# A feed-forward down product computed in seven block products, with the sums of its weights made by DMA beforehand

## The chip, the cores and the metric

The kernel runs on one core of a Trainium2 chip. The metric is the time of one execution on the device in microseconds. The median of three runs of the kernel before is 3528.7 us (3525.08 to 3528.71).

## What is computed

Three transformer-like blocks run one after the other on a sequence of 1024 tokens with 1024 features, all in 32-bit floating point. Each ends in a feed-forward part, called f1, f2 and f3 here. The change touches that of the third block, f3, whose reference is cut to this:

```python
h = rms_norm_3(x, norm2_pre)               # and a modulation of its rows
f = jnp.square(jax.nn.relu(h @ w_fc1)) @ w_fc2     # 1024 -> 4096 -> 1024
x = x + g2 * rms_norm_3(f, norm2_post)     # g2: a gate per feature
```

The product with `w_fc1` is called up, that with `w_fc2` down.

## The kernel before

**Products.** Every 32-bit operand is split into a high and a low part: ScalarE copies the high part (`whi` or `Hh`, line 319) and VectorE subtracts it from the operand to give the low part (`wlo` or `Hl`, line 305). A product is then three matmuls, high by high, high by low and low by high (`mm3`, line 324). A tile of 128 by 1024 numbers, 512 KB, is one unit.

**The stream of units.** The object `W` holds all weights in the order in which they are wanted. SyncE's queue loads units into four buffers named `raw` (`drop_raws` leaves two of them), two units ahead of the split; the split writes them into six slots in SBUF. A unit is split as soon as a slot is free, and its `raw` buffer is free after that.

**Up (`up7`, line 896).** The product is cut into 2 by 2 blocks and made from seven block products in place of eight. Sums of weight blocks are made on VectorE in the `raw` buffers (`raw<-raw`), sums of the input blocks beforehand (`t`). There are 16 groups for f3. The first product of the first 12 (`FIRST`) is made in a loop ahead and kept in DRAM (`sd`), so 60 matmuls are left in each of these groups and 84 in the last four. The results of a group are four tiles of 128 by 512 in 8 slots of `X`; ScalarE applies relu and square to each and writes it to DRAM (`gd`) through its own DMA queue. GpSimd's queue brings the kept products back (line 963, `X<-sdf`). Four banks of PSUM hold the products (`mm`).

**Down (`down7`, line 1028).** For f3 the 32 tiles of `gd` come back as units and are split into `Hh` and `Hl`. They are worked off in chunks of 2, 2 and seven times 4 tiles (`CHUNKS`). Per chunk there are 8 column blocks and two halves of the tokens; VectorE adds each result to `X` (`X<-X,mm`). In the last chunk the second half of the tokens is cut in two quarters (`PARTS`), each followed by its own `tail`: the norm, the gate, the residual `xr` (read back from DRAM, `xd`) and the store of the output on SyncE's queue.

**The order.** A scheduler orders the instructions of each engine by priorities; the order on an engine is not that of the source. Each engine runs its list in order and stops where a semaphore is not there yet. `W.tick` is called all along the source; `pe` is a count of TensorE time kept while the program is built.

Of the kernel before, what the change touches and what calls it, by code (L numbers as in the profile page):

```python
# [57 lines left out]

def _feat(a):

    return np.ascontiguousarray(a.T.reshape(KT, P, a.shape[0]).transpose(1, 0, 2))


def lay_out(i):
# [42 lines left out]
    a["w3_down"] = i["w_fc2_3"].reshape(32, P, D)  # L107
# [40 lines left out]
class Stream:  # L148
# [5 lines left out]
    def __init__(self, k):  # L154
        self.k = k
        self.seq = []
        self.nd = self.ns = 0
        self.free = {"A": 4, "B": 0}
        self.pools = {}
        self.bphase = ()  # L160
        self.raws = []
        self.groom = [False, False]
# [40 lines left out]
    def _split(self):  # L203
# [38 lines left out]
        while self.nd < min(self.ns + 2, len(self.seq)):  # L242
# [23 lines left out]


class Kern:
    def __init__(self, tc, a, out):
        self.tc, self.nc, self.a, self.out = tc, tc.nc, a, out  # L270
        self.bgs = []
        self.due = {}
        self.pe = 0.0
        self.clk = {tc.nc.vector: 0.0, tc.nc.scalar: 0.0, tc.nc.gpsimd: 0.0}
        self.stacks = []
        self.ada_pend = []
        self.adap = None

# [372 lines left out]

    CHUNKS = {"f1": [2, 2] + [4] * 7, "f2": [2] + [4] * 5, "f3": [2, 2] + [4] * 7}

# [4 lines left out]
    def setup(self):  # L658
# [46 lines left out]
        def ffn7(n, up, down, with_ada=0):  # L705
# [19 lines left out]
            S[n + "h"], S[n + "d"] = [], []  # L725
            gd = S[n + "x"] = self.drp.tile([a[down].shape[0], P, T], F32, name="gd" + n)
# [168 lines left out]
    def up7(self, name):  # L895
# [3 lines left out]
        gated = name == "f2"  # L899
# [7 lines left out]
        def relu2(dst, src, m, t, scale=1.0):  # L907
            self.act(dst, src, AF.Relu, scale=scale)
            self.act(dst, dst, AF.Square)
            nc.scalar.dma_start(out=gd[m, :, 512 * t:512 * t + 512], in_=dst)  # L910
# [12 lines left out]
        for g in range(0, M, 2):  # L923
# [7 lines left out]
            for i in (0, 1):  # L931
                u = first[g + i]
                self.part7(u, 512, H[1, 0], ps[i], False)
                W.done(u)
                s = scratch()
                if gated:
                    self.act(s, ps[i], AF.Copy)
                    nc.scalar.dma_start(out=cd[g + i], in_=s)
                else:
                    relu2(s, ps[i], 2 * (g + i), 0)  # L940
# [7 lines left out]
        def slot():  # L948
            n[0] += 1
            return X1[:, (n[0] - 1) % 8]  # L950
# [6 lines left out]
        def start(g):  # L957

            ca = wide() if gated else None
            s1 = None  # L960
            if g < M:
                s1 = scratch() if gated else slot()
                nc.gpsimd.dma_start(out=s1, in_=sd[g])
                if gated:
                    nc.gpsimd.dma_start(out=ca[:, :512], in_=cd[g])
            return s1, ca

        nxt = start(0)
        for g, G in enumerate(groups):
# [18 lines left out]
            if g >= M:  # L988
# [4 lines left out]
                else:  # L993
                    relu2(slot(), z, 2 * g, 0)
# [11 lines left out]
            if not gated:  # L1006
                relu2(c22, c22, 2 * g + 1, 1)
# [4 lines left out]
            else:  # L1012
                relu2(c21, c21, 2 * g + 1, 0)
# [9 lines left out]
            else:  # L1023
                relu2(v, v, 2 * g, 1)
        W.groom[1] = True
        self.ext_es.close()
        self.open_ss()

    def down7(self, name, add, tail, quarters=False):
# [4 lines left out]
        residual = 0 if name == "f3" else 4  # L1034
# [478 lines left out]
    def block2(self):  # L1513
# [243 lines left out]

        self.up7("f2")
# [268 lines left out]
    def block3(self):  # L2027
# [204 lines left out]
        self.hp, e = self.pool("hp2", 1, None, "right")  # L2232
        self.ffn_es.insert(0, e)
        ac = []

        def add(m, part, ps, first, last):
            half, c0, c1 = part
            o = c0 - half * 512
            x = self.X[half][:, m, o:o + c1 - c0]
            if first:  # L2240
                self.act(x, ps, AF.Copy)
            else:
                self.tt(x, x, ps, ALU.add)
            if last:
                if m == 0 and o == 0:
                    ac.append(self.acc())
                if m == 0 and not xr:
                    take_slots()
                self.sq_add(ac[half], x, m, o)

        xr = []

        def take_slots():

            ts = []
            for q in "AB":
                while W.free[q] and len(ts) < 8:
                    W.free[q] -= 1
                    for n in ("hi", "lo"):
                        t = W.pools[q].tile([P, UW], F32R, tag=n, name="xr").bitcast(F32)[:, :T]  # L2260
                        t = t.rearrange("p (a b) -> p a b", b=512)
                        k = len(ts)
                        self.dma(t, self.xd[:, k:k + 2, 0:512])
                        ts.extend((t[:, 0], t[:, 1]))
            xr.append(ts)

        def tail(part):
# [3 lines left out]
            if half and len(xr) < 2:  # L2271
                t = self.hp.tile([P, KT, 512], F32, tag="h0", name="xr")
                self.dma(t, self.xd[:, :, 512:])
                xr.append([t[:, k] for k in range(KT)])
# [7 lines left out]
            for k in range(KT + 1):  # L2282
# [3 lines left out]
                if k:  # L2286
                    f = self.X[half][:, k - 1, o:o + n]
                    x = xr[half][k - 1]
                    self.tt(f, f, x[:, o:o + n], ALU.add, gp if not half or k % 2 else None)
# [4 lines left out]
        self.down7("f3", add, tail, quarters=True)  # L2294
# [30 lines left out]
```

## Time and profile before

| | |
|---|---|
| median of three runs | 3528.7 us |
| profiled execution | 3526.44 us |
| its span | 3524.6 us |
| TensorE busy | 3419.4 us, 97% |
| VectorE busy | 2201.8 us, 62% |
| ScalarE busy | 1367.4 us, 39% |
| GpSimd busy | 335.8 us, 10% |
| mean rate of DMA | 120 GB/s |

The span is the time from the first to the last instruction in the profiled execution. Busy time counts instructions, not waits. The stages that matter here, by the trace: f2 up from about 1750 to 2300 us, f2 down to about 2480, the third block's other work to 2868, f3 up to 3146, f3 down to the end.

### The profile page before, as it was taken

How to read it: one execution, taken by the hardware profiler on the slowest of the kernel's cores; microseconds unless marked ns; L12 is line 12 of the kernel's file. 1: busy time of each engine (PE TensorE's matmuls, PEld its weight loads, DVE VectorE, ACT ScalarE, POOL GpSimd, SP SyncE). 2: the span in 40 equal slices, each digit the busy share in tenths (PEclk: the TensorE clock that was granted, in tenths of full speed). 3: DMA queues.
4: the chain of work that ended last, by engine and by line, in shares of the span. 5: the costliest groups of instructions: out<-in, count | busy, mean ns of one | idle time of the engine just before them, and what ended most of it. 6: DMA issues, size and time to landing. Idle time of an engine off the chain costs nothing. (4 is left out here: it accounts for less than half of the span.)

```text
span 3524.6 us, 43683 instructions
## 1 busy us (share of the span) xinstructions
PE 3419.4 (97%) x16725; PEld 2808.1 (80%) x16725; DVE 2201.8 (62%) x3747; ACT 1367.4 (39%) x2046; POOL 335.8 (10%) x368
## 2 busy tenths in 40 slices
PE   7999999999999989999999999999999999999998
PEld 7788898887888777876698788878778878877887
DVE  5456366556666574667768988867665676645444
ACT  3432244444112443555634444431332564451111
POOL 0111020000000210000020000000232410000003
PEclk9999999999999999998999999999999999999999
DMA  3111444336633186444325322274222154343222
GB/s 106 48 43 47 148 135 148 117 118 191 184 133 113 58 196 173 123 129 147 110 94 166 116 84 84 96 221 149 88 67 90 62 184 149 132 167 114 96 84 72
DMA packets 180964, 421.46 MB, mean 120 GB/s; under 512 B 18088, under 2 KB 58744, under 8 KB 180628
## 3 DMA queue, kind: packets, MB, share of 16 engines
q1 hardware_dynamic: 133044, 325.34, 28.8%
q10 hardware_dynamic: 38304, 67.13, 5.1%
q0 software_dynamic: 9408, 26.22, 3.6%
q8 instruction: 131, 2.15, 0.3%
q14 instruction: 77, 0.63, 0.1%
HBM read 304.50 MB, written 105.63 MB: 116 GB/s over the span
## 5 line engine op out<-in xcount | busy, mean ns | idle before, releaser
L324 PE MATMUL mm<-Hh,whi 128*128 128x512 f32 (+3 forms) x3632 | 1384.2, 381 | 11.7 <-DVE X L305 4.5
L324 PE MATMUL mm<-Hh,wlo 128*128 128x512 f32 (+3 forms) x3632 | 1365.6, 377 | 4.7 <-DVE wlo L305 4.7
L324 PE MATMUL mm<-Hl,whi 128*128 128x512 f32 (+3 forms) x3632 | 1369.6, 377 | 0.2 <-DVE Hl L305 0.2
L324 PEld LDWEIGHTS mm<-Hh,whi 128*128 128x128 f32 x3632 | 686.0, 189 | 155.3 <-issue 6.8
L324 PEld LDWEIGHTS mm<-Hh,wlo 128*128 128x128 f32 x3632 | 685.7, 189 | 138.5 <-DVE wlo L305 9.0
L324 PEld LDWEIGHTS mm<-Hl,whi 128*128 128x128 f32 x3632 | 686.1, 189 | 127.7 <-issue 1.4
L319 ACT ACTIVATE whi<-raw 128x1024 fp32r<-128x1024 f32 (+3 forms) x386 | 379.0, 992 | 694.6 <-PE mm L324 459.9
L305 DVE TENSOR_TENSOR wlo<-raw,whi 128x1024 fp32r<-128x1024 f32 (+3 forms) x386 | 441.7, 1151 | 193.3 <-ACT whi L319 182.8
L305 DVE TENSOR_TENSOR X<-X,mm 128x512 f32<-128x512 f32 (+1 forms) x446 | 290.3, 655 | 366.7 <-PE mm L324 362.1
L324 PE MATMUL mm<-t,whi 128*128 128x512 f32 x1296 | 408.6, 396 | 2.4 <-ACT whi L319 2.4
L324 PEld LDWEIGHTS mm<-t,whi 128*128 128x128 f32 x1296 | 242.9, 188 | 62.4 <-ACT whi L319 3.3
L324 PE MATMUL mm<-t,wlo 128*128 128x512 f32 x648 | 256.7, 396 | 1.9 <-DVE wlo L305 1.7
L319 ACT ACTIVATE Hh<-raw 128x1024 fp32r<-128x1024 f32 x86 | 89.6, 1057 | 364.8 <-PE mm L324 213.3
L321 ACT ACTIVATE X<-X 128x512 f32<-128x512 f32 (+1 forms) x226 | 151.9, 673 | 186.2 <-DVE X L310 153.7
L305 POOL TENSOR_TENSOR acc<-acc,sq 128x256 f32<-128x256 f32 (+1 forms) x108 | 115.9, 1074 | 910.0 <-ACT sq L321 906.4
L305 DVE TENSOR_TENSOR raw<-raw 128x512 f32<-128x512 f32 x216 | 145.2, 687 | 79.5 <-DMA raw<-in_w_up 77.1
L324 PEld LDWEIGHTS mm<-t,wlo 128*128 128x128 f32 x648 | 121.8, 188 | 33.4 <-DVE wlo L305 4.1
L305 DVE TENSOR_TENSOR Hl<-raw,Hh 128x1024 fp32r<-128x1024 f32 x86 | 104.6, 1222 | 56.9 <-ACT Hh L319 56.3
L310 DVE SCALAR_TENSOR_TENSOR ada<-raw,silc,ada 128x128 f32<-128x128 f32 x336 | 115.5, 350 | 8.3
L324 PE MATMUL mm<-whi,Hh 128*128 128x264 f32 (+4 forms) x336 | 111.7, 342 | 6.5 <-ACT Hh L319 2.8
L324 PE MATMUL mm<-wlo,Hh 128*128 128x264 f32 (+4 forms) x336 | 111.2, 340 | 2.4 <-DVE wlo L305 2.4
L310 DVE SCALAR_TENSOR_TENSOR X<-mm,X 128x512 f32<-128x512 f32 x108 | 74.5, 690 | 61.6 <-PE mm L324 60.1
(290 smaller groups left out, 3400.0 us busy)
## 6 DMA issues: line engine op xcount, KB each, us to landing
raw<-in_w_up SPq DMA_DIRECT2D x136, 512.0 KB
raw<-gdf SPq DMA_DIRECT2D x86, 512.0 KB
raw<-in_w_down SPq DMA_DIRECT2D x86, 512.0 KB
gdf<-X ACTq DMA_DIRECT2D x108, 256.0 KB
raw<-in_w_ada SPq DMA_DIRECT2D x48, 512.0 KB
gdf<-X ACTq DMA_DIRECT2D x22, 512.0 KB
B<-qd SPq DMA_DIRECT2D x36, 256.0 KB
A<-qd SPq DMA_DIRECT2D x36, 256.0 KB
```

The lines of the kernel that those rows point to most:

```text
L305: eng.tensor_tensor(out=out, in0=a, in1=b, op=op)
L310: self.nc.vector.scalar_tensor_tensor(out=out, in0=a, scalar=s, in1=b, op0=op0, op1=op1)
L319: self.nc.scalar.activation(out, in_, f, scale=scale, **kw)
L321: self.nc.scalar.activation(out, in_, f, bias=bias, scale=scale, **kw)
L324: self.nc.tensor.matmul(out, l, r, start=s, stop=e, skip_group_check=grp)
```

## The change

Only the down product of f3 is put differently, with what it needs ahead of it.

- `w_fc2` is laid out by 2 by 2 blocks (`_quarters`). The product is made from seven block products, P1, P2, P6, P7, P4, P5 and P3 in this order, each in 8 steps of 24 matmuls; in each step a unit of weights and a unit of the activations are streamed and split. P1 with P2, P6 with P7 and P5 with P3 share their sums in PSUM (`down_parts`). VectorE and ScalarE touch a result only at a product's last step. The stream may run four units ahead in place of two, except in P3.
- Four of the products want sums of weight blocks. `sums` makes these in DRAM, one each 24 us of counted time from f2's up stage on: 16 copies of 1 MB from DRAM to DRAM on ScalarE's queue, kept in source order there, and 16 accumulating DMAs of 1 MB on GpSimd's queue.
- Four of the products want sums of activations. `up7` makes these for f3 with four more VectorE operations per group and writes four tiles per group through GpSimd's queue; one tile that ScalarE wrote earlier is read back per group. Sixteen slots of `X` are used in place of eight.
- The residual is read with two DMAs of 2 MB on GpSimd's queue into `Hh` at the start of the down stage. The second half of the tokens has one tail of 512 columns in place of two of 256.

```diff
+    def sums(self, name, w, pace, at):
+        S = self.S[name + "s"]
+        late = []
+        for i, q, p in ((0, 1, 3), (1, 0, None), (2, 1, 0), (3, 2, None)):
+            for e in range(4):
+                r = slice(2 * e, 2 * e + 2)
+                self.sums_todo.append((self.nc.scalar, S[i, r], w[e, q], {}))
+                self.sums_todo += late
+                src = w[e, p] if p is not None else S[0 if i == 1 else 1, r]
+                late = [(self.nc.gpsimd, S[i, r], src, dict(accum_op=ALU.add, max_dma_last_dim=4096))]
+        self.sums_todo += late
...
+    def sums_step(self):
+        if self.sums_todo and self.pe >= self.sums_at:
+            eng, dst, src, kw = self.sums_todo.pop(0)
+            ins = eng.dma_start(out=dst, in_=src, **kw)
+            if not kw:
+                self.tc.keep_in_program_order(ins)
+            self.sums_at = self.pe + self.sums_pace
...
     def tick(self):
         self.k.ada_flush()
+        self.k.sums_step()
...
+                elif parts:
+                    nc.gpsimd.dma_start(out=ca, in_=piece(0, g))
...
-                relu2(v, v, 2 * g, 1)
+                if parts:
+                    relu2(v, v)
+                    t1_, t2_, t4_ = slot(), slot(), slot()
+                    self.tt(t1_, ca, v, ALU.subtract)
+                    self.tt(v, c22, v, ALU.subtract)
+                    self.stt(t2_, t1_, -1.0, c22, ALU.mult, ALU.subtract)
+                    self.stt(t4_, t2_, -1.0, c21, ALU.mult, ALU.subtract)
+                    for i, t in ((3, t1_), (5, v), (4, t2_), (6, t4_)):
+                        nc.gpsimd.dma_start(out=piece(i, g), in_=t)
...
+    def down_parts(self, name, out, tail):
...
+        W.ahead = 4
+        new = True
+        for n, i in enumerate(self.ORDER):
+            if n == 6:
+                self.drop_raws()
+                W.ahead = 2
+            if new:
+                ps = [self.ps() for _ in range(4)]
+            for e in range(8):
+                wa, wb = (W.get(u) for u in D_[8 * n + e])
+                for m in range(4):
+                    for k in (0, 1):
+                        w, x = slice(k * 512 + m * P, k * 512 + m * P + P), slice(k * 512, k * 512 + 512)
+                        self.mm3(ps[m], wa.hi[:, w], wa.lo[:, w], wb.hi[:, x], wb.lo[:, x],
+                                 new and e == 0 and k == 0, e == 7 and k == 1, not new)
...
+                    if e == 7:
+                        z = ps[m]
+                        if i == "P1":
+                            self.act(s[:, m], z, AF.Copy)
+                        elif i == "P2":
+                            out(0, m, z, 1)
+                        elif i == "P6":
+                            self.tt(v[:, m], z, s[:, m], ALU.add)
...
+            new = i not in ("P1", "P6", "P5")
+            if i == "P4":
+                self.unsummed = True
+                self.norms[0] = self.bg(tail((0, 0, 512)))
+            elif i == "P3":
+                self.unsummed = True
+                self.norms[1] = self.bg(tail((1, 512, 1024)))
...
+        self.sums("f3", a["w3_down"], 24.0, 0.0)
         self.up7("f2")
...
         self.open_ring("f3d")
...
+        xr = self.Hh.bitcast(F32)
+        for k in (0, 4):
+            nc.gpsimd.dma_start(out=xr[:, k:k + 4, :T], in_=self.xd[:, k:k + 4])
...
-        self.down7("f3", add, tail, quarters=True)
+        self.down_parts("f3", out, tail)
```

VectorE's list in the middle of f3's up stage, one group of the kernel before. `raw<-raw` are the sums of weights, `wlo` the low parts, and `X<-mm,X` with `X<-X,mm` what becomes of the products:

```order
2690 L305 TENSOR_TENSOR raw<-raw 128x512 x2
2691 L305 TENSOR_TENSOR X_21489<-mm,X_21489 128x512
2692 L305 TENSOR_TENSOR raw<-raw 128x512
2693 L305 TENSOR_TENSOR wlo<-raw,whi 128x1024
2694 L305 TENSOR_TENSOR raw<-raw 128x512
2695 L305 TENSOR_TENSOR wlo<-raw,whi 128x1024
2696 L305 TENSOR_TENSOR X_21489<-mm,X_21489 128x512
2697 L310 SCALAR_TENSOR_TENSOR X_21489<-mm,X_21489 128x512 x2
2698 L305 TENSOR_TENSOR wlo<-raw,whi 128x512
2699 L305 TENSOR_TENSOR X_21489<-X_21489,mm 128x512
```

One group of the changed kernel at the same place, on the same engine:

```order
2650 L318 TENSOR_TENSOR raw<-raw 128x512
2651 L318 TENSOR_TENSOR X_21521<-X_21521,mm 128x512
2652 L318 TENSOR_TENSOR raw<-raw 128x512 x3
2653 L318 TENSOR_TENSOR wlo<-raw,whi 128x1024
2654 L318 TENSOR_TENSOR X_21520<-X_21520,X_21521 128x512
2655 L318 TENSOR_TENSOR wlo<-raw,whi 128x1024
2656 L318 TENSOR_TENSOR X_21520<-X_21521,X_21520 128x512
2657 L323 SCALAR_TENSOR_TENSOR X_21520<-X_21520 128x512
2658 L318 TENSOR_TENSOR X_21520<-mm,X_21521 128x512
2659 L323 SCALAR_TENSOR_TENSOR X_21520<-X_21520,X_21521 128x512
2660 L318 TENSOR_TENSOR X_21520<-mm,X_21521 128x512
2661 L318 TENSOR_TENSOR wlo<-raw,whi 128x512
```

The four new operations are those from `X` alone, without `mm`. The first addition of a product, `X<-mm,X`, stood behind two `raw<-raw` (2691) and stands behind all four, both wide `wlo` and three of the new operations now (2658).

SyncE's list where f3's up stage ends and its down stage begins, before; `in_w_up` and `in_w_down` are the weights, `gdf` the activations, and `xr` the residual:

```order
391 L183 DMA raw<-gdf_102 128x1024
392 L183 DMA raw<-in_w_up 128x1024
393 L183 DMA raw<-in_w_down 128x1024 x2
394 L183 DMA raw<-gdf_102 128x1024 x3
395 L328 DMA xr<-xd 128x8x512
396 L183 DMA raw<-in_w_down 128x1024 x2
```

The same place in the changed kernel:

```order
395 L191 DMA raw<-in_w_down 128x1024
396 L191 DMA raw<-in_w_up 128x1024
397 L191 DMA raw<-gdf_102 128x1024
398 L191 DMA raw<-in_w_down 128x1024
399 L191 DMA raw<-gdf_102 128x1024
400 L191 DMA raw<-in_w_down 128x1024
```

Weights and activations take turns now, one unit each per step, and the residual has left SyncE's list.

## Rows read from the trace of the kernel before

**Rows 1.** the page's line of engines, whole span.

```profile
PE 3419.4 (97%) x16725; PEld 2808.1 (80%) x16725; DVE 2201.8 (62%) x3747; ACT 1367.4 (39%) x2046; POOL 335.8 (10%) x368
```

**Rows 2.** windows over the down stage of f3, the first line names the columns.

```profile
core 0: us, PE busy (x) PEld busy (x) DVE busy (x) ACT busy (x) POOL busy (x), PEclk, DMA share, GB/s
3146.00:3187.00 41.00, 37.73 (x159) 29.14 (x159) 24.54 (x27) 22.52 (x31) 0.00 (x0) 1.00 0.73 255
...
3269.00:3310.00 41.00, 41.00 (x179) 33.13 (x178) 19.30 (x23) 8.16 (x8) 0.00 (x0) 1.00 0.31 103
...
3351.00:3392.00 41.00, 41.00 (x178) 33.08 (x177) 19.41 (x23) 8.15 (x8) 0.00 (x0) 1.00 0.32 103
```

**Rows 3.** waits of TensorE, f3 down; columns: us in total, times, longest.

```profile
PE mm L324 <- ACT X L319: 1.8, 1, 1.8
PE mm L324 <- DVE X L305: 1.2, 1, 1.2
```

**Rows 4.** chain of waits at the end: start, us, what.

```profile
3504.09 4.39 PE mm L324 x36
...
3518.10 0.78 DVE X L310 x2
```

**Rows 5.** windows of f2 up, f2 down and f3 up, columns as in rows 2.

```profile
1900.00:1980.00 80.00, 77.58 (x330) 60.94 (x329) 72.42 (x86) 31.95 (x31) 4.85 (x9) 1.00 0.38 125
1980.00:2060.00 80.00, 78.11 (x335) 62.46 (x334) 74.79 (x88) 36.58 (x39) 0.54 (x1) 1.00 0.29 104
2060.00:2140.00 80.00, 80.00 (x346) 64.59 (x345) 65.90 (x74) 34.08 (x37) 0.00 (x0) 1.00 0.23 79
...
2300.00:2360.00 60.00, 56.37 (x247) 44.85 (x246) 40.07 (x86) 17.33 (x19) 4.35 (x4) 1.00 0.72 205
2360.00:2420.00 60.00, 58.19 (x255) 46.85 (x254) 40.01 (x82) 10.29 (x10) 0.81 (x1) 1.00 0.65 195
...
2920.00:3000.00 80.00, 80.00 (x346) 64.47 (x345) 49.78 (x69) 37.13 (x53) 2.82 (x6) 1.00 0.46 153
```

**Rows 6.** timeline of VectorE, f3 up: start, us, operation, idle before.

```profile
2965.15 0.68 DVE L305 TENSOR_TENSOR wlo<-raw,whi 128x512 fp32r<-128x512 f32 x1
...
2969.94 1.42 DVE L305 TENSOR_TENSOR raw<-raw 128x512 f32<-128x512 f32 x2 [1.92 <-DMA raw<-in_w_up]
2971.27 0.68 DVE L305 TENSOR_TENSOR X<-mm,X 128x512 f32<-128x512 f32 x1
2971.87 0.68 DVE L305 TENSOR_TENSOR raw<-raw 128x512 f32<-128x512 f32 x1
2972.55 1.23 DVE L305 TENSOR_TENSOR wlo<-raw,whi 128x1024 fp32r<-128x1024 f32 x1
2973.69 0.68 DVE L305 TENSOR_TENSOR raw<-raw 128x512 f32<-128x512 f32 x1
```

**Rows 7.** GpSimd's sdf loads in f3 up (timeline), then that line's landing.

```profile
2916.10 0.54 POOL L963 DMA_DIRECT2D X<-sdf  x1 [39.06 <-DVE X L305]
...
3013.84 0.54 POOL L963 DMA_DIRECT2D X<-sdf  x1 [13.43 <-DMA gdf<-X]
...
DMA to landing us min/median/max: 2.7/3.2/6.2
```

**Rows 8.** accumulating loads of 1 MB, line 1066: issue in ns, landing.

```profile
L1066 POOL DMA_DIRECT2D X<-xd x8: 1273/1281/1348, 865.2 to 2359.5; - x8
...
DMA to landing us min/median/max: 10.4/13.7/17.2
```

**Rows 9.** groups by line and shape, 3146 to 3525: busy us, mean ns.

```profile
L305 DVE TENSOR_TENSOR wlo<-raw,whi 128x1024 fp32r<-128x1024 f32 x31 | 37.4, 1223 | 19.6 <-ACT whi L319 19.6
L319 ACT ACTIVATE whi<-raw 128x1024 fp32r<-128x1024 f32 x31 | 32.1, 1054 | 95.5 <-PE mm L324 66.7 <-DMA raw<-in_w_down 28.6
L310 DVE SCALAR_TENSOR_TENSOR X<-X,gp,ax 128x512 f32<-128x512 f32 x8 | 5.8, 742 | 1.2 <-PE ax L324 1.2
```

More of the change, by code (lines that the diff above doesn't have):

```diff
@@ L161, in __init__ @@
         self.raws = []
+        self.ahead = 2
         self.groom = [False, False]
@@ L241, in _split @@
         self.ns += 1
-        while self.nd < min(self.ns + 2, len(self.seq)):
+        while self.nd < min(self.ns + self.ahead, len(self.seq)):
             self.load()
@@ L905, in up7, with piece, relu2 @@
                       Hl[:, 4 * j:4 * j + 4, 512 * t:512 * t + 512]) for j in (0, 1) for t in (0, 1)}
-        def relu2(dst, src, m, t, scale=1.0):
-            self.act(dst, src, AF.Relu, scale=scale)
+        def piece(i, g):
+            if parts:
+                return gd[i, g // 2, :, g % 2]
+            h = 512 * (i > 1)
+            return gd[2 * g + (i in (1, 2)), :, h:h + 512]
+        def relu2(dst, src, i=None, g=None):
+            self.act(dst, src, AF.Relu)
             self.act(dst, dst, AF.Square)
-            nc.scalar.dma_start(out=gd[m, :, 512 * t:512 * t + 512], in_=dst)
+            if i is not None:
+                nc.scalar.dma_start(out=piece(i, g), in_=dst)
         def conv(y, c, j):
@@ L957, in start @@
         def start(g):
-            ca = wide() if gated else None
+            ca = wide() if gated else slot() if parts else None
             s1 = None
@@ L1032, in down7 @@
         D_, Gu = self.S[name + "d"], self.S[name + "h"]
-        residual = 0 if name == "f3" else 4
+        residual = 4
         c = 0
@@ L2231, in block3, with out @@
         self.open_ring("f3d")
-        self.hp, e = self.pool("hp2", 1, None, "right")
-        self.ffn_es.insert(0, e)
+        xr = self.Hh.bitcast(F32)
+        for k in (0, 4):
+            nc.gpsimd.dma_start(out=xr[:, k:k + 4, :T], in_=self.xd[:, k:k + 4])
         ac = []
[L2236 to L2241, printed above, removed]
-            else:
[L2243 to L2265, printed above, removed]
+        got = [0, 0]
+        def out(half, m, z, sign, extra=None):
+            x = self.X[half][:, m]
+            if extra is None:
+                self.act(x, z, AF.Copy)
+            elif sign > 0:
+                self.tt(x, z, extra, ALU.add)
+            else:
+                self.stt(x, z, -1.0, extra, ALU.mult, ALU.subtract)
+            if not got[half]:
+                ac.append(self.acc())
+            self.sq_add(ac[half], x, got[half])
+            got[half] += 1
         def tail(part):
@@ L2270, in tail @@
             self.unsummed = False
[L2271 to L2274, printed above, removed]
             yield self.after(1.0)
@@ L2287, in tail @@
                     f = self.X[half][:, k - 1, o:o + n]
-                    x = xr[half][k - 1]
-                    self.tt(f, f, x[:, o:o + n], ALU.add, gp if not half or k % 2 else None)
+                    self.tt(f, f, xr[:, k - 1, c0:c1], ALU.add, gp if not half or k % 2 else None)
                     self.dma(self.out[:, k - 1, c0:c1], f)
```

62 lines of the change are left out of this document (55 added, 7 removed).

## The prediction

> **What bounds the kernel now.** I began with the page's engine line: TensorE is busy 3419.4 of 3524.6 us [rows 1], so a change can pay by removing matmuls or cost by making TensorE wait; nothing else shows in the time. The table of windows over the down stage of f3, from 3146 us on, then gives the rate. Its inner rows are full, 41.00 of 41.00 us, with 178 or 179 matmuls: 82 us over 357 matmuls is 0.2297 us each [rows 2]. Only the first window is short of work, 37.73 of 41.00, with the DMA engines at a share of 0.73 [rows 2], and the view of waits names what it was: ScalarE's and VectorE's writes to X, 1.8 and 1.2 us [rows 3]. The chain of waits gives the end: the last product is the piece of 4.39 us that begins at 3504.09, so it ends at 3508.48, and after it come some 16 us of norm, residual and store, of which VectorE's last scalings, on 256 columns, take 0.39 each [rows 4]. In the windows of f3's up stage TensorE is full as well (80.00 of 80.00) while VectorE works 49.78 [rows 5]: a cover of 30 us in 80 for new VectorE work, if the order lets it be used.
>
> **What is removed.** The down product had 32 k-tiles x 8 column blocks x 2 halves x 3 = 1536 matmuls of 512 columns (the last 192 cut in 256s). Now there are 7 products x 8 steps x 24 = 1344. That is 192 fewer, all on TensorE, which is full there: 192 x 0.2297 = **-44.1 us**. The stage lasted 3508.48 - 3146 = 362.5 us against 1536 x 0.2297 = 352.8, so 9.7 us went to the first window's 3.3, the norm's small matmuls and the 256-column pieces. The pieces go, and the first two pairs of units are split before the up stage ends, since the new code may run four loads ahead. I take **-4** of these 9.7, with 0 and -9 as ends, because the residual's 4 MB now load at the same moment from GpSimd's queue.
>
> **What is added in the down stage.** Both operands are now streamed: 112 units are split where 64 were, 48 x 1054 ns more on ScalarE and 48 x 1223 on VectorE [rows 9]. Per step of 24 matmuls, 5.51 us, that is 2 x 1054 = 2.1 us and 2 x 1223 = 2.4, while the 120 additions X<-X,mm on VectorE fall to a few per product; both engines have room and I cost it at nothing. The cover is the stock of three pairs of slots (six); if it is gone, the loads set the pace, the third rival. At the end the norm's last pass is on 512 columns in place of 256. With 742 ns for a 512-wide pass [rows 9] against 0.39 [rows 4], eight of these make +2.8, the added residual on VectorE and the longer first square +1.2: **+4**, between +2 and +6. GpSimd's 512-wide residual additions run beside it.
>
> **What is added in the up stage of f3.** This is the term on which the forecast turns. Each of 16 groups gets four VectorE operations of 512 columns, four stores and one more load, the last five on GpSimd's queue, at 0.54 us of issue each [rows 7]: 6 x 0.54 = 3.2 us in a group of 13.96 (3013.84 - 2916.10 over seven issues), hidden. VectorE's load rises by 4 x 0.60 to 0.69, from about 8.7 to 11.4 us a group: still under the period. But the order says where the four stand. Before, the addition that TensorE's third block product waits for (X<-mm,X) came right behind the first two additions on raw and was done 2.0 us after the load had landed (2971.27 + 0.69 - 2969.94) [rows 6]. Now it is behind three more raw operations, two wide wlo and two of the four new ones. That closes a ring. From the end of wlo 128x512 to the landing of the next load the timeline shows 2969.94 - 2965.83 = 4.1 [rows 6]. Then follow raw 0.60, the v addition 0.60, three raw 1.80, wlo 1.14, new 0.60, wlo 1.14, new 0.60 and 0.60, the addition 0.73 (starts of neighbours in rows 6 are 0.60 apart for 512 columns, 1.14 for 1024), 12 matmuls of the third product 2.95 until its bank is read, the next addition 0.62 and wlo 0.68: 16.2 us. A group of 60 matmuls took 13.96, so 2.2 us a group where the ring is closed. By the order that holds for seven groups; 7 x 2.2 = 15, and 3 more for the groups before them, whose ring is shorter. **+18.** The upper end, if each load takes 1.5 us longer because six small transfers per group share its path (the sdf loads already land between 2.7 and 6.2 us [rows 7]), is 7 x 3.7 + 6 = +32. The lower end comes from f2, whose groups keep VectorE at 72.42 and 74.79 of 80 us and lose 2.42 and 1.89 us of TensorE, and at 65.90 (82%, what 11.4 of 13.96 would be) lose none [rows 5]: by that rate 12 groups cost between 0 and 3.0% of 168 us, 5; I set this end at +4. I take the ring, not f2's rate, since f2's order does not have the ring.
>
> The Trainium skill ("DMA: Bandwidth & Descriptors", section "Anatomy of one DMA") puts a transfer at about 2.0 us plus its bytes at 436 GB/s, written for GpSimd's queue; an estimate by that page for 512 KB is 3.2 us. The trace shows 4.1 with the wait for issue in it, on SyncE's queue, so I keep the row; by the page the ring would be 15.3 us and the term +12, the time 3499.
>
> **What is added before.** From f2's up stage on, 16 copies and 16 accumulations of 1 MB stand one every 24 us of counted TensorE time; 32 x 24 = 768 of a count that takes 0.2133 us for a matmul (512 / 2400), 827 at the trace's 0.2297. The first stand near 1890, so the last near 2720, well ahead of their first reader past 3230. The accumulation's nearest row is X<-xd, 1 MB: issue 1.28 us, landing 13.7 (10.4 to 17.2) [rows 8]. ScalarE and GpSimd lose only issue time, behind which no product waits. What they can cost is weight loads that arrive late: in f2's down stage the DMA engines are at 0.72 and 0.65 and TensorE already loses 3.63 and 1.81 us of 60 [rows 5]; about seven of the 32 fall there. The scheduler also orders f2 and block 3 slightly otherwise. Between -2 and +20, I take **+4**, near the rows' loss of 5.4 us that a busy DMA costs there today.
>
> **Sum.** -44.1 - 4 + 4 + 18 + 4 = -22.1 on the profiled execution of 3526.4 gives 3504.3; the median of the runs shown is 2.3 higher than that execution, and half of it goes on top: **3505 us**. By the low ends it is near 3480, with all high ends near 3540. About 0.2%, 7 us, is what a measurement can tell from no change, so "faster" means under 3521.6 and "slower" over 3535.8.
>
> **Rival 1, the ring is covered.** If loads land sooner or the engines run the four operations in gaps that a static order doesn't show, the up term is +4 as by f2's rows and the time 3505 - 14 = 3491. For it: VectorE idles 30 of 80 us there [rows 5]. Against: its idle time sits in front of loads and of TensorE [rows 6], where the ring has none to give.
>
> **Rival 2, the sums disturb f2.** 32 transfers of 10 to 17 us each cover about 400 us of the 827. If they hold back one load in four by another 4 us, that is 8 to 16 us in f2's up stage, where TensorE already loses 2.42 in 80 at a share of 0.38, and the loss in the down stage doubles, 5.4: +20 in place of +4, so 3521, between 3512 and 3531. For it: the windows with most DMA are those with lost TensorE time [rows 5]. Against: at 0.46, f3's up loses nothing. The Trainium skill (same page, section "Queues, rings and completion order") says that each DMA engine takes its queues in turn, packet by packet, by which a load beside a copy and an accumulation would get a third; the slower landings beside other traffic in rows 7 agree in direction, and no row has three queues at work.
>
> **Rival 3, loads set the pace of the down stage; slower than before.** A step needs 1.05 MB in 5.51 us, 190 GB/s. With four raw buffers a round of two steps is 11.03 us, of which the split holds the last buffer 1.05 + 1.22 [rows 9]; the four loads have 8.8 us, 2.10 MB, 239 GB/s. That is the point from which it decides. The first window delivered 255 [rows 2], f2's down stage 205 and 195 [rows 5]. At 205 a round takes 10.2 + 2.3 = 12.5, each of 56 steps 0.74 more, +41: 3546. Against: those rates came with the DMA engines at 0.65 to 0.73, not full, so they show what was asked for more than what can be had; the steady stage moves 103 GB/s at 0.31 [rows 2], which scales to 0.57 for 190.
>
> **Chances.** The forecast 0.48 (3497 to 3513), rival 1 0.20 (3485 to 3496), rival 2 0.17, rival 3 0.11, and 0.04 for what I have not seen, such as sums that are read before they are ready. Faster: 0.47 + 0.20 + 0.09 = 0.76. Same: 0.01 + 0.07 and 0.03 of the rest = 0.11. Slower: 0.11 + 0.01 + 0.01 = 0.13. The range 3487 to 3530 leaves out about 0.05 below and 0.13 above.
>
> **What would show it.** The distance of the group's loads on GpSimd in f3's up stage should be about 16.2 us in the seven inner groups, with TensorE waiting for X of VectorE near 2 us in each; 13.9 to 14.3 there means rival 1. The down stage should last 315 to 322 us to its last matmul, with full windows at 24 matmuls in 5.51 us and a DMA share near 0.6; waits of TensorE for whi or wlo released by DMA mean rival 3. The first of the evenly spaced loads there, at 2916.10 before [rows 7], should come within 8 us of that; 15 or more later means rival 2. The forecast fails most plainly if the up stage keeps its period, or if the inner windows of the down stage are not full.

## The result and the profile after

The changed kernel takes 3591.2 us (median of four runs, 3587.0 to 3594.1) against 3527.7 us before: a ratio of 1.018, with a 95% interval of 1.0167 to 1.0192. It is slower by 64 us; 3505 us and a gain of 22 were forecast, and the time lies outside the range. The profiled execution has a span of 3592.3 us, against 3524.6 before.

The page's line of engines answers to [rows 1]. TensorE has 288 recorded matmuls fewer and is busy 10.2 us less, not 44:

```profile
PE 3409.2 (95%) x16437; PEld 2785.2 (78%) x16437; DVE 2220.8 (62%) x3725; ACT 1407.9 (39%) x2079; POOL 396.5 (11%) x452
```

I cut both executions at the same places of the program: ScalarE's first store of `sd` in f3's up stage (2825.58 before, 2917.16 after), the first matmul of f3's down product (3146 and 3254.36), its last matmul (3508.48 and 3570.21) and the end. The store belongs to the loop that makes the first products ahead of the groups, so f3's up stage begins near 2826 in the kernel before; the 2868 given above for its start lies within it.

| from, to | before | after | difference | forecast |
|---|---|---|---|---|
| start to the first store of f3's up stage | 2825.6 | 2917.2 | **+91.6** | +4 |
| to the first matmul of the down product | 320.4 | 337.2 | +16.8 | +18 |
| to its last matmul | 362.5 | 315.9 | -46.6 | -48.1 |
| to the end of the span | 16.1 | 22.1 | +6.0 | +4 |
| sum | 3524.6 | 3592.3 | +67.7 | -22.1 |

Three of the four lines came out within 2 us. The whole miss is in the first line, in stages whose arithmetic the change does not touch.

**The down product.** The windows over it (columns as in rows 2) are full from the start; the loads delivered up to 306 GB/s where they were wanted, and settle near 186; the view of TensorE's waits has no line in this stage:

```profile
3260.00:3300.00 40.00, 40.00 (x173) 32.27 (x172) 18.31 (x16) 17.12 (x18) 0.54 (x1) 1.00 0.85 306
3300.00:3340.00 40.00, 40.00 (x173) 32.25 (x173) 17.32 (x15) 15.43 (x17) 0.00 (x0) 1.00 0.56 186
...
3500.00:3540.00 40.00, 40.00 (x173) 32.24 (x172) 26.27 (x20) 16.57 (x18) 10.17 (x6) 1.00 0.64 211
```

**Before f3.** The same kind of windows over the four stretches ahead of f3's up stage, cut at the first load of f2's down weights, the store of `xd` behind f2's down product, the first `w<-zb` of block 3 and the store named above. Before:

```profile
1840.00:2257.28 417.28, 412.97 (x1800) 332.54 (x1799) 354.02 (x411) 183.32 (x205) 14.71 (x22) 1.00 0.32 108
2257.28:2508.30 251.02, 245.14 (x1070) 197.06 (x1069) 169.54 (x316) 68.61 (x78) 9.05 (x8) 1.00 0.52 162
2508.30:2616.10 107.80, 102.01 (x439) 83.81 (x438) 67.77 (x127) 53.00 (x78) 32.87 (x28) 0.91 0.22 75
2616.10:2825.58 209.48, 206.25 (x1140) 175.27 (x1140) 118.27 (x187) 78.59 (x160) 74.46 (x78) 1.00 0.23 79
```

After:

```profile
1840.00:2295.89 455.89, 425.05 (x1807) 340.78 (x1806) 353.44 (x413) 182.89 (x207) 22.13 (x31) 0.96 0.45 136
2295.89:2567.34 271.45, 253.13 (x1067) 200.78 (x1066) 166.37 (x316) 68.60 (x78) 12.19 (x11) 0.97 0.63 180
2567.34:2700.87 133.53, 105.88 (x442) 85.90 (x441) 65.07 (x127) 55.74 (x80) 35.62 (x30) 0.83 0.31 94
2700.87:2917.16 216.29, 208.60 (x1140) 176.23 (x1140) 118.65 (x187) 77.44 (x160) 75.24 (x80) 0.99 0.31 95
```

The counts of instructions on TensorE agree within seven in each stretch, and up to that store both traces hold the same 13716 matmuls, so the work is the same. The stretches are longer by 38.6, 20.4, 25.7 and 6.8 us, which is the 91.6. TensorE's idle time (first number less second) rises from 19.2 to 84.5 us, +65.3; the other 26.3 is the matmuls taking longer, with a granted clock of 0.83 to 0.99 of full speed where it was 0.91 to 1.00.

The view of TensorE's waits from 1840 us to that store names few large ones (columns: us in total, times, longest). After:

```profile
PE ax L337 <- POOL acc L318: 18.9, 4, 17.2
PE mm L337 <- ACT whi L332: 14.2, 4, 9.1
PE mm L337 <- DVE wlo L318: 11.7, 12, 2.4
PE mm L337 <- ACT t L332: 10.5, 1, 10.5
```

Before, over the same part of the program, the first of these is small and the last does not occur:

```profile
PE mm L324 <- DVE wlo L305: 5.9, 5, 2.2
PE mm L324 <- DVE X L305: 3.3, 3, 1.5
PE ax L324 <- DVE rr L305: 2.9, 3, 1.1
PE mm L324 <- ACT whi L319: 2.4, 2, 1.3
PE ax L324 <- POOL acc L305: 2.4, 3, 1.4
```

The timeline of GpSimd shows the wait of 17.2 from the other side. Columns: start, us, engine, line, operation, and in brackets the idle time before with what ended it:

```profile
2607.24 0.45 POOL L318 TENSOR_TENSOR ws<-ws,tril 128x128 f32<-128x128 f32 x1 [43.67 <-DMA tril<-in_tril]
2607.66 1.26 POOL L318 TENSOR_TENSOR acc<-acc,sq 128x512 f32<-128x512 f32 x1
2608.87 0.46 POOL L318 TENSOR_TENSOR ws<-ws,tril 128x128 f32<-128x128 f32 x1
...
2613.14 0.90 POOL L685 DMA_DIRECT2D swf<-swf  x1
2613.75 3.26 POOL L318 TENSOR_TENSOR acc<-acc,sq 128x512 f32<-128x512 f32 x2
```

Before, the same two operations stood the other way round:

```profile
2556.65 1.72 POOL L305 TENSOR_TENSOR acc<-acc,sq 128x512 f32<-128x512 f32 x1
2558.32 2.14 POOL L305 TENSOR_TENSOR ws<-ws,tril 128x128 f32<-128x128 f32 x4
```

`ws<-ws,tril` belongs to the spatial mixing of block 3 and waits for the load of `tril`, which SyncE issued at 2601.52; `acc` is the sum of squares for which TensorE's next norm waits. In the new list `acc` stands behind it, and behind one of the new accumulations. Nothing in the diff mentions either. The scheduler had put the lists of f2 and block 3 in another order: by the two traces some 400 of the 3226 instructions of VectorE ahead of the store stand elsewhere in its list, and TensorE's list differs too. The question for the runs was how much of the 91.6 us is that order, and how much the traffic of 32 transfers of 1 MB.

### The profile page after: what moved, and what is told of

The parts are those of the page before. It is cut to its first block, busy times and chain, and to the rows that moved or that the text cites. A ratio compares the mean times of both kernels' runs of the same rounds, so it can differ in the third digit from the quotient of the medians.

```text
span 3592.3 us, 43348 instructions
## 1 busy us (share of the span) xinstructions
PE 3409.2 (95%) x16437; PEld 2785.2 (78%) x16437; DVE 2220.8 (62%) x3725; ACT 1407.9 (39%) x2079; POOL 396.5 (11%) x452
## 4 chain that ended last, share of the span: by engine, by line
PE 49%; DVE 9%; DMA 5%; issue 2%; ACT 2%; POOL 1%; SPq 0%; DVEq 0%; ACTq 0%; POOLq 0%
PE mm L337 41%; PE ax L337 5%; PE o L337 2%; DVE X L318 1%; DMA raw<-in_w_up 1%; DVE wlo L318 1%; DVE X L323 1%; DMA cb<-cs 1%; DMA raw<-in_w_ada 1%; DVE raw L318 1%; DVE ca L323 1%; POOL acc L318 1%; DVE acc L318 0%; DMA raw<-gdf 0%; DMA raw<-in_w_down 0%
## 5 line engine op out<-in xcount | busy, mean ns | idle before, releaser
L337 PE MATMUL mm<-Hh,whi 128*128 128x512 f32 (+3 forms) x3088 | 1182.5, 384 | 29.8 <-DVE X L318 16.2
L337 PE MATMUL mm<-Hh,wlo 128*128 128x512 f32 (+3 forms) x3088 | 1165.7, 378 | 14.4 <-DVE wlo L318 14.4
L337 PE MATMUL mm<-Hl,whi 128*128 128x512 f32 (+3 forms) x3088 | 1168.8, 379 | 2.3 <-DVE Hl L318 2.3
L318 DVE TENSOR_TENSOR wlo<-raw,whi 128x1024 fp32r<-128x1024 f32 (+3 forms) x466 | 544.9, 1181 | 337.3 <-ACT whi L332 331.2
L337 PEld LDWEIGHTS mm<-Hh,whi 128*128 128x128 f32 x3088 | 587.4, 190 | 156.2 <-DVE X L318 21.6
L337 PEld LDWEIGHTS mm<-Hl,whi 128*128 128x128 f32 x3088 | 587.5, 190 | 110.0 <-DVE Hl L318 3.4
L318 DVE TENSOR_TENSOR raw<-raw 128x512 f32<-128x512 f32 x216 | 143.1, 687 | 79.8 <-DMA raw<-in_w_up 78.3
L318 POOL TENSOR_TENSOR acc<-acc,sq 128x512 f32<-128x512 f32 (+1 forms) x102 | 117.0, 1148 | 682.4 <-ACT sq L334 673.9
L337 PE MATMUL mm<-whi,wlo 128*128 128x512 f32 x448 | 177.0, 395 | 0.0
L337 PE MATMUL mm<-wlo,whi 128*128 128x512 f32 x448 | 176.9, 395 | 0.0
L337 PE MATMUL mm<-whi 128*128 128x512 f32 x448 | 176.8, 395 | 0.0
```

Source lines behind the costliest of these rows:

```text
L318: eng.tensor_tensor(out=out, in0=a, in1=b, op=op)
L337: self.nc.tensor.matmul(out, l, r, start=s, stop=e, skip_group_check=grp)
```

## The experiments

In each title stands the name under which the expectation was recorded. "Store" is the first store of `sd` in f3's up stage in the profiled execution, 2825.6 before and 2917.2 after. Ratios are to the kernel before, run beside it on the same chip.

**e_nosums: the changed kernel without the sums.**

```diff
-                A.update({"P5": sw[0], "P6": sw[1], "P7": sw[2], "P3": sw[3]})
+                A.update({i: [a[down][e // 2, q, e % 2] for e in range(8)]
+                          for i, q in (("P5", 1), ("P6", 0), ("P7", 2), ("P3", 3))})
...
-        self.sums("f3", a["w3_down"], 24.0, 0.0)
```

> The changed kernel without its weight sums: no copies and no accumulations, and the four products that want sums read plain quarters of the weights in their place, so that part of the result is left out. All else is as changed, and every engine's list up to f3's up stage is that of the kernel before. By the traces the changed kernel loses 91.6 us ahead of f3's up stage, loses 16.8 in it and gains 40.6 behind it. If the sums are the whole cause of the 91.6 (theory), this kernel gives 3527.7 + 16.8 - 40.6 = 3504, within 5. If something else of the change reaches back into f2 and block 3 (rival), it stays above 3540.

3499.6 us, 0.992 [0.9902, 0.9931]; store at 2826.0; f3's up stage 336.0 us. All of the loss ahead of f3 comes with the sums, and the rest of the change saves 27 us against the kernel before beside it.

**e_before_sums: the kernel before, with the sums.**

```diff
+        self.sums("f3", a["w3_down"], 24.0, 0.0)
```

(with `sums`, `sums_step` and the DRAM they write, which no product reads)

> The kernel before with the 32 copies and accumulations added at the same pace and places, into DRAM that nobody reads. Theory, the sums alone make the loss ahead of f3: 3527.7 + 91.6 = 3619, within 8, with the losses near 1960, 2600 us. Rival, the loss comes from the sums together with the new f3 code: under 3560.

3618.7 us, 1.026 [1.0242, 1.0272]; store at 2915.2. The sums alone cost the kernel before the same 90 us, and by the traces they put its lists in the changed kernel's order up to the store.

**e_order32: the changed kernel with sums of 32 KB.**

```diff
-                self.sums_todo.append((self.nc.scalar, S[i, r], w[e, q], {}))
+                self.sums_todo.append((self.nc.scalar, S[i, 2 * e:2 * e + 1, 0:8], w[e, q][0:1, 0:8], {}))
...
```

(the accumulations likewise; the products read plain quarters as in e_nosums)

> As e_nosums, with the list of 32 copies and accumulations back but 32 KB long in place of 1 MB, read by nobody (the products read plain quarters, so that part of the result is left out). That is 1 MB of traffic where the change has 32, yet the scheduler still orders f2 and block 3 otherwise than before. Theory A, the other order makes the loss: 30 to 100 us over e_nosums, 3535 to 3605. Theory B, the traffic of the sums makes it: within 6 of e_nosums, about 3504 to 3510.

3536.3 us in one run; store at 2860.6, 35 us late with a thirty-second of the bytes. The smaller transfers also changed the scheduler's order once more, so this run says that order matters, not how much. The next two pin the order.

**x_order_before: all of the sums' bytes, in the order that the lists have with sums of 1 KB.** With 1 KB the scheduler leaves f2 and block 3 in the order of before. The kernel is built with 1 KB, its list on each engine is read off, and the full kernel is built with these lists as constraints.

```diff
+                    for p, q in zip(seq, seq[1:]):
+                        tc.add_manual_dep(traced[q], traced[p].name, mybir.DependencyInfo(
+                            mybir.DependencyClass.NoSync, mybir.DependencyReason.DATA), reason="order")
...
+    nc, order = build("tiny", None)
+    nc, got = build("full", order)
```

> The changed kernel with all its sums, 1 MB copies and accumulations that the products read, and its whole result. Only the order differs: every engine's list is the one that the scheduler gives when the same 32 transfers are 1 KB long, which up to f3 is the order of the kernel before with the transfers slipped in. Theory A, the scheduler's other order makes the loss ahead of f3: 3500 to 3510, as e_nosums. Theory B, the traffic makes it: about 3592. Mixed, 37 us of order as e_order32 had and the rest traffic: 3545 to 3560.

3512.8 us, 0.996 [0.9943, 0.9972]; store at 2837.4. The median of seven runs (3500.5 to 3520.2) is 3 us above theory A's range and far from B's. The trace bears the order out: up to the store TensorE, VectorE, GpSimd and SyncE run the same sequence as in the kernel before, the sums' transfers set aside. What the bytes still cost shows in VectorE's waits for loads in f2 (from 1840 us to just behind its down stage, 2540 and 2530; this run first, then e_nosums):

```profile
DVE raw L318 <- DMA raw<-in_w_up: 13.1, 5, 8.1
DVE raw L318 <- DMA raw<-in_w_up: 5.2, 4, 3.8
```

**x_order_after: the other corner, the changed kernel's own lists with 1 KB transfers.**

```diff
-    nc, order = build("tiny", None)
-    nc, got = build("full", order)
+    nc, order = build("full", None)
+    nc, got = build("tiny", order)
```

(against x_order_before; the products also read plain quarters as in e_nosums)

> The opposite: each engine's list word for word as in the changed kernel, but the 32 transfers 1 KB long and read by nobody (the products read plain quarters, so that part of the result is left out). Theory A, order: 3580 to 3592, the changed kernel's time nearly whole. Theory B, traffic: 3500 to 3510. Mixed: 3535 to 3560.

3571.7 us, 1.013 [1.0115, 1.0145]; store at 2899.4. That is 8 us below theory A's range and far above the others. The waits of the changed kernel are there with hardly any traffic (TensorE, from 1840 us to the store):

```profile
PE ax L337 <- POOL acc L318: 19.7, 4, 18.0
PE mm L337 <- DVE wlo L318: 12.9, 12, 2.9
PE mm L337 <- ACT whi L332: 10.0, 4, 5.7
PE mm L337 <- ACT t L332: 9.9, 1, 9.9
```

With e_nosums and the changed kernel the square is closed. Time of the store, us:

| | lists as before | lists as changed | order |
|---|---|---|---|
| next to no bytes | 2826.0 (no sums) | 2899.4 | +73.4 |
| all bytes | 2837.4 | 2917.2 | +79.8 |
| traffic | +11.4 | +17.8 | +91.2 |

Four fifths of the loss ahead of f3 is order, one fifth traffic. Each entry is one profiled execution, and executions with the same lists and bytes differ by up to 4 us at the store (2826.0 in e_nosums and 2830.3 in e_tlate below; 2837.4, 2838.9 and 2839.1 in x_order_before, c_six and c_edit2), so the traffic is known to some 4 us. The medians of the whole times give the same picture: order 72 and 78 us, traffic 13 and 20. In the left column, traffic also contains the issue of the transfers, which e_nosums doesn't have.

**a_ws: the changed kernel, block 3's `ws<-ws,tril` behind `acc`.**

```diff
+    pool = order["EngineType.Pool"]
+    ws = [n for w, g, n in Kern.MARKS if w == "ws"]
+    k = pool.index(ws[0])
+    for n in ws:
+        pool.remove(n)
+    pool[k + 14:k + 14] = ws
```

> The changed kernel in its own order of instructions, with one thing moved: the four ws<-ws,tril of block 3 stand fourteen places later in GpSimd's list, behind the additions to acc as in the kernel before, so that they no longer hold acc back while tril is being loaded. Theory (the order of the lists, not the traffic, makes block 3's start late): the wait of PE ax for POOL acc, 17.2 us from 2599 to 2617 in the changed kernel's trace, goes, and with it 17 to 25 us (the slow clock behind the gap included): 3567 to 3575 us, f3 up 17 to 25 us earlier than its 2917. Rival (the copies' traffic or another wait stands behind it): something else ends last there and the time stays within 4 us of 3591.

3588.3 us, 1.017 [1.0151, 1.0185]: a miss, the rival's figure. GpSimd's timeline shows why:

```profile
2601.01 1.27 POOL L318 TENSOR_TENSOR acc<-acc,sq 128x512 f32<-128x512 f32 x1 [30.97 <-ACT sq L334]
2610.12 0.89 POOL L695 DMA_DIRECT2D swf<-swf  x1 [7.83 <-DMA swf<-in_w_down]
2610.72 2.92 POOL L318 TENSOR_TENSOR acc<-acc,sq 128x512 f32<-128x512 f32 x2
```

One of the new accumulations stands between the additions to `acc` and waits for its copy, which ScalarE had issued at 2599.70. Two waits lay over each other, and the second took the first one's place: TensorE's wait was 16.7 us in place of 17.2.

**a_ws2: that accumulation (marked "acc" in the list) moved behind the additions as well.**

```diff
+    mv = ws + [n for n in pool[k:k + 10] if ("acc", n) in [(w, m) for w, g, m in Kern.MARKS]]
...
-    pool[k + 14:k + 14] = ws
+    pool[k + 14:k + 14] = mv
```

(against a_ws)

> a_ws with one more instruction moved: the accumulation swf<-swf that stands between the additions to acc at block 3's start, where GpSimd waited 7.83 us for its copy in a_ws (until 2610.12), goes behind them too, together with the four ws<-ws,tril. Theory (an accumulation queued on GpSimd took over the wait that the moved ws<-ws,tril gave up): PE's wait for POOL acc, 16.7 us in a_ws, goes, and 12 to 25 us with it: 3563 to 3576 us. Rival (a third thing stands behind it): within 4 us of a_ws's 3588.

3585.1 us, 1.016 [1.0145, 1.0179]; store at 2906.2. The wait of TensorE falls to 8.7 us, and what ends GpSimd's idle time there is now ScalarE's square:

```profile
2599.87 4.62 POOL L318 TENSOR_TENSOR acc<-acc,sq 128x512 f32<-128x512 f32 x3 [31.02 <-ACT sq L334]
2608.92 2.60 POOL L318 TENSOR_TENSOR acc<-acc,sq 128x512 f32<-128x512 f32 x2 [4.43 <-ACT acc L334]
```

By the median it saves 3 us against a_ws and 6 against the changed kernel, so by the time it is the rival's figure; in the profiled execution the wait is halved and the span is 10.8 us shorter than a_ws's. The stretch of block 3 is 127.3 us in place of 133.5, where it was 107.8 before. What is left may be order too, which no run isolates: TensorE's sums of squares came in two pieces with products around them before (16 matmuls at 2558.42, 16 at 2562.85), and here come as one piece of 32 with a wait on either side.

**a_t: the changed kernel, f2's four `X<-X,X` ahead of the waiting `raw<-raw`.** In the changed kernel's f2, VectorE runs the four operations that ScalarE's `t` needs only at 1900.93, behind four `raw<-raw` that waited 6.03 us for a load; before, they ran from 1864.64 on. `stt` are these four; `late` stands for the copies of ScalarE that go with them. After, then before:

```profile
1897.25 2.62 DVE L318 TENSOR_TENSOR raw<-raw 128x512 f32<-128x512 f32 x4 [6.03 <-DMA raw<-in_w_up]
...
1900.93 4.63 DVE L323 SCALAR_TENSOR_TENSOR X<-X,X 128x1024 f32<-128x1024 f32 x4
```

```profile
1864.64 1.21 DVE L310 SCALAR_TENSOR_TENSOR X<-X,X 128x1024 f32<-128x1024 f32 x1
```

```diff
...
+    for n in stt:
+        dve.remove(n)
+    j = dve.index(before[-1]) + 1
+    dve[j:j] = stt
+    late = [n for n in lo if n not in before]
+    k = act.index(late[0] - 1)
+    for n in late:
+        act.remove(n - 1)
+    act[k - 3:k - 3] = [n - 1 for n in late]
```

> The changed kernel in its own order of instructions, with one thing moved: at the start of f2's up product the four X<-X,X that ScalarE's t waits for stand ahead of the raw<-raw that waits for a load of in_w_up on VectorE, and ScalarE's four copies ahead of its whi that waits. Theory (VectorE's list holds t back): PE's wait for ACT t near 1890 to 1902 us, 10.5 us, goes, and the slow clock behind it, so f2's down product starts 8 to 20 us earlier than its 2295.89 and the time is 3571 to 3583 us. Rival (the load that comes late is needed just behind anyway, so PE waits for whi in place of t): within 4 us of 3591.

3581.2 us, 1.015 [1.0135, 1.0166]: 10 us less than the changed kernel, within what was expected. But the place is less clear than the size: TensorE still waits 5.6 us there, now for VectorE's `t`, and f2's up stretch is 450.5 us, not far below the 451.7 and 453.1 that it has in a_ws and a_ws2, where nothing was moved in it. The down stage of f2 starts 5.4 us earlier than the changed kernel's, short of the 8 to 20 expected. The wait is not gone because VectorE's own `t<-X,t`, which the edit does not move, still stand behind the load:

```profile
1893.73 2.62 DVE L318 TENSOR_TENSOR raw<-raw 128x512 f32<-128x512 f32 x4 [4.17 <-DMA raw<-in_w_up]
1896.28 1.23 DVE L318 TENSOR_TENSOR wlo<-raw,whi 128x1024 fp32r<-128x1024 f32 x1
1897.42 4.62 DVE L318 TENSOR_TENSOR t<-X,t 128x1024 fp32r<-128x1024 f32 x4
```

**a_all: both edits.**

```diff
+    pool[k + 14:k + 14] = mv
...
+    dve[j:j] = stt
...
+    act[k - 3:k - 3] = [n - 1 for n in late]
```

> a_ws2 and a_t together, whose places lie 600 us apart: if each wait is paid for by itself, the gains add, a_t's 10 us to a_ws2's 12 to 25: 3553 to 3566 us. Rival (what one saves, the other's load or copy takes back): no more than the larger of the two alone.

3582.7 us, 1.015 [1.0139, 1.0169]: the gains do not add. The rival holds, no more than the larger of the two. Both waits are as short as in the single edits (8.7 us for `acc`, 5.2 for `t`), yet f2's up stretch is 454.5 us with a_t's edit in it, no shorter than without, so a_t's gain can't be placed in that stretch; what both runs with the edit share is a shorter down stretch of f2 (267.0 and 267.4 us, where the changed kernel, a_ws and a_ws2 have 270.8 to 273.5), and why is open. So mending these two waits does not bring back the order's 73 to 80 us. That the loss is spread over many places, with a wait that goes uncovering the next, is a reading of this and not shown. Which of the many moved instructions costs what is left open.

**c_six: x_order_before, with one slot less per group in f3's up stage.** This is about the other term, +16.8 in f3. A group takes 7 of 16 slots of `X`, so the slot of the next `v` is one that the four new operations still read, and the addition for which TensorE waits cannot go ahead of them. The edit is on top of x_order_before, whose up stage lasts 331.1 us, so 6.1 of the 16.8 have gone there with the other lists.

```diff
-                    t1_, t2_, t4_ = slot(), slot(), slot()
+                    t1_, t2_, t4_ = ca, slot(), slot()
```

> As x_order_before, whole result, with one edit in f3's up stage: the first of a group's four new operations writes over the tile that was read back, so a group takes six of the 16 slots of X and not seven. With seven, the slot of a group's first addition is that of a tile which the four new operations of the group before still read, so the addition cannot stand ahead of them; with six it can, and in the list it does. Theory, the slots close the ring: groups of 14.0 to 14.8 us and 8 to 15 less than x_order_before. Rival, the work itself is too much for VectorE: period above 15.8, within 4 of x_order_before.

3505.9 us, 0.994 [0.9925, 0.9955]; f3's up stage 327.4 us. The gain of 6.9 us by the medians, 3.7 in the stage, is short of the 8 to 15 expected, and the inner groups come 15.0 us apart, between the theory's 14.0 to 14.8 and the rival's 15.8. The slot alone is a part of the cause.

**c_edit2: with the slot free, the four operations moved in VectorE's list.** The first two go behind `wlo` 128x512 of the next group, the other two behind that group's addition for `v`, in seven groups.

```diff
+        behind(t[0], dve[p])
+        behind(t[1], t[0])
+        behind(t[2], M["vadd"][g + 1])
+        behind(t[3], t[2])
```

> As c_six, with VectorE's list of seven inner groups edited: two of the four new operations stand behind wlo 128x512 and two behind the addition to v, where VectorE waits for the next load. If the ring is all that holds the groups, the period is 13.9 to 14.2 there, as before, and the time 2 to 6 below c_six; if the stores on GpSimd's queue or slower loads hold them too, no gain over c_six.

3497.4 us, 0.992 [0.9907, 0.9936]: it beats both kernels, with the whole change in it. It is 8.5 us below c_six, more than the 2 to 6 expected. The inner groups come 14.0 us apart, f3's up stage is 320.3 us, the 320.4 of before, and TensorE's longest waits from 2825 to 3254 us, which hold it, are:

```profile
PE mm L346 <- ACT whi L336: 3.4, 1, 3.4
PE mm L346 <- DVE wlo L322: 2.8, 3, 1.2
PE mm L346 <- DVE X L327: 1.9, 2, 1.0
```

**e_tlate: the same aim through the source, with the four operations written behind the next group's additions (without the sums).**

```diff
-                    self.tt(t1_, ca, v, ALU.subtract)
...
+                    late.append((g, ca, v, c22, c21))
```

> As e_nosums (plain quarters of the weights, so that part of the result is left out), with the four VectorE operations of a group in f3's up stage written behind the next group's products, so that they no longer stand ahead of the addition that TensorE waits for. If the ring makes the 16.5 us period of the changed kernel's groups (theory), the period falls to 14.0 to 14.5 and the time to 12 to 16 below e_nosums, about 3490. If VectorE's added work or the stores on GpSimd's queue make it (rival), the period stays above 15.5 and the time within 5 of e_nosums.

3506.9 us, 0.993 [0.9911, 0.9947], 7 us above e_nosums where 12 to 16 less were expected: TensorE waited 12.3 us for X, as much as the 12.2 in e_nosums. Source order does not set the list, so this run decides nothing about the ring.

## Why the prediction was wrong, point by point

**What is removed: right.** 1344 matmuls at 0.2297 are 308.7 us, and the down product lasted 315.9. The stage shrank by 46.6 for a forecast of 48.1; of the 9.7 us that it had beyond its matmuls, 7.2 stayed, so the -4 was -2.5.

**What is added in the down stage: right.** Splitting 112 units cost nothing, as the full windows show. The tail is 6.0 longer, the upper end of the 2 to 6 given. Rival 3 is refuted: its point of decision was 239 GB/s, and an early window delivered 306 with TensorE full. At a steady 186 GB/s the DMA engines are at 0.56, the 0.57 that the scaling from [rows 2] gave.

**What is added in the up stage: right, with its mechanism.** GpSimd's first stores of eight inner groups stand from 3041.05 to 3156.54, 16.5 us apart; 16.2 was worked out from the ring. TensorE's wait for X of VectorE in the stage, none before, is 12.1 us in 14 waits; near 2 us in each of seven groups was forecast. The wait, and one round of the ring on VectorE:

```profile
PE mm L337 <- DVE X L318: 12.1, 14, 2.1
```

```profile
3113.65 0.68 DVE L318 TENSOR_TENSOR wlo<-raw,whi 128x512 fp32r<-128x512 f32 x1
...
3119.05 0.69 DVE L318 TENSOR_TENSOR raw<-raw 128x512 f32<-128x512 f32 x1 [3.39 <-DMA raw<-in_w_up]
```

That is 4.7 us from the end of `wlo` to the landing; a round earlier it is 3.6 (3098.47 to 3102.03), and the 4.1 of [rows 6] lies between them. By the Trainium skill ("DMA: Bandwidth & Descriptors", section "Anatomy of one DMA") an estimate for such a load was 3.2 and the round 15.3; the measured round is on the side of the row. c_six and c_edit2 show the cause directly: with a slot free (-3.7 us) and the four operations elsewhere (-7.1) the rest of the term is gone, and rival 1's price (a covered ring) is what a better order gives.

**What is added before: this step failed.** +4, between -2 and +20, was 91.6. Two things were wrong in it. The first is a size: the traffic costs 11.4 us in the old order and 17.8 in the new, in the upper half of its range and not near the 5.4 of [rows 5]. Of rival 2, this much was right: loads are held back, as VectorE's waits for `in_w_up` show (13.1 us in place of 5.2), at a price between its +20 and the +4. The Trainium skill (same page, section "Queues, rings and completion order") has the engines take their queues in turn, by which a load beside a copy and an accumulation is slowed; the +11.4 with the order held fixed agrees in direction, and no run here separates the share per queue.

The second is the sentence "The scheduler also orders f2 and block 3 slightly otherwise", which got no price and no rival of its own. It is worth 73 to 80 us. The listing of the order was read closely in f3, where the change was meant to be, and hardly in f2 and block 3, where it was only passed over. There the new places of `acc` behind `ws<-ws,tril`, of the accumulations between them, and of the `X<-X,X` behind a waiting `raw<-raw` could have been seen, each on an engine that runs its list in order, each behind an instruction that waits for a load or a copy. Seeing them would not have priced them: moving the first two back is worth 3 to 6 us by the median (a_ws, a_ws2). "ScalarE and GpSimd lose only issue time, behind which no product waits" was false on GpSimd: eight of the accumulations kept it waiting 269.8 us in all for their copies, which cost nothing where nothing urgent stood behind, and `acc` of block 3's norm stood behind another one, which held it for 7.8 us in a_ws. From the view of the line that issues them:

```profile
  DMA swf<-in_w_down: 269.8, 8
...
DMA to landing us min/median/max: 8.2/8.9/20.8
```

**The landmark** named as a test did its work: "15 or more later means rival 2" was 95 later, 3011.22 for 2916.10. But it could not tell loads held back from lists put otherwise, since rival 2 was written with one mechanism only; it took the 2 x 2 of order and bytes to do that.

## What to carry to other kernels

A scheduler that orders by priorities can move instructions far from the edit when DMAs are added, and each engine stops at the first one that waits: compare the lists of every stage in which anything was added, and give an order that differs a price of its own. The waits that one sees there don't add up to it, as a_all shows, so the price is best measured. To tell what a change costs by its work from what it costs by its order, pin the order and change the bytes, then the other way round. Where the order is the loss, pinning the good one can be enough: here the same change with pinned lists, one slot saved and four operations moved takes 3497 us in place of 3591.

## What the runs showed of the hardware

Behind TensorE's gaps the granted clock fell, and stayed low after the work came back. In the changed kernel (columns as in rows 2):

```profile
2580.00:2600.00 20.00, 19.82 (x86) 15.73 (x84) 6.19 (x9) 2.46 (x3) 0.00 (x0) 1.00 0.25 91
2600.00:2620.00 20.00, 2.94 (x14) 2.94 (x14) 5.72 (x6) 5.75 (x10) 9.69 (x11) 0.59 0.85 254
2620.00:2640.00 20.00, 13.46 (x49) 11.63 (x50) 11.78 (x30) 11.12 (x18) 6.78 (x5) 0.56 0.06 12
2640.00:2660.00 20.00, 17.89 (x74) 14.47 (x73) 7.90 (x20) 11.65 (x17) 6.83 (x5) 0.78 0.00 1
```

TensorE was nearly idle for 17 us, and the next 40 us were run at 0.56 and 0.78 on the mean, where 1.00 is 2.4 GHz and 0.50 is 1.2. Slower matmuls of this kind are the 26 us by which 65 us of added waits became 92 us of time ahead of f3.

The 16 accumulations of 1 MB from DRAM to DRAM landed in 8.9 us (median; 8.2 to 20.8), less than the 13.7 of the nearest row, [rows 8], that had stood for them; the trace has no landings for the copies. So these transfers were faster than assumed and the loss was larger, in line with a loss that is mostly not of the bytes.
